# x loaded behind the embeddings' weights, gates on column tiles, two small steps moved: a change to a two-layer decoder trunk

## The chip, the cores and the metric

The kernel runs on one core of a Trainium2 chip. The metric is device time in microseconds (us) of one execution. The engines are called as the profile calls them: PE (TensorE matmul), PEld (its weight loads), DVE (VectorE), ACT (ScalarE), POOL (GpSimd), SP (SyncE, which issues most DMAs).

## The reference

256 tokens of width 2048 go through two layers. Everything is f32.

```
h = x
for i in 0, 1:
    hn = rmsnorm(h)
    if i == 0:                                   # even layer
        q, f, i, z, xb, zb = split(hn @ e_w_in)  # six blocks of 1024
        ya = head_rmsnorm(hgrn2(q, f, i)) * silu(z)       # gated linear recurrence, 8 heads of 128
        xc = causal_conv(xb)                               # 4 taps
        yb = rg_lru(xc) * silu(zb)   # r, i = sigmoid(xc @ block-diagonal), a = exp(-8 r softplus(-lam))
        h += concat(ya, yb) @ e_w_out
    else:                                        # odd layer
        qk, v, og, z, ig, fg = split(hn @ o_w_in)  # ig, fg: one column for each of 8 heads
        q, k = silu(causal_conv(qk))
        li, lf = ig + c_b_i, log_sigmoid(fg + c_b_f)
        yc = head_rmsnorm(mlstm(q, k, v, li, lf)) * sigmoid(og) * silu(z)  # cumulative sums and running
        h += yc @ o_w_out                                                    # maxima of li, lf weight q k^T
    h += sigmoid(h @ ple_gate_w[i]) * rmsnorm(p[i] @ ple_w[i])   # p: per-layer embeddings, width 256
return rmsnorm(h)
```

## The kernel before

About 200 MB of f32 weights pass once through the core. `load_weights` (L113) fetches a 1 MB tile of weights in two halves on SP's queue (L122), ACT casts each half to a rounded type (L124, `whi`), and DVE subtracts to get the low part (L125, `wlo`). Activations are split the same way (`ahl`: L139 and L140 for p, L277 and L278 with the norm's gain). Every product with a large weight is then three products, high by high, high by low, low by high. `block` does it for one column block of 128 outputs and all 256 tokens: sixteen matmuls at L155, a `pump()`, sixteen at L161. `project_tok` does it for 512 outputs with tokens on the partitions (L196, L197, L198), four quarters of the weight, a `pump()` in each.

The order of the work around these streams is written by hand. Side work is put into generators, in lanes (`start("par", ...)`, `"norm"`, `"att"`, `"rg"`, `"mix"`, `"fm"`). Each `pump()` advances every lane by one step up to its next `yield`, and holds what it issues behind the latest main instruction of PE, ACT and DVE (`tc.issue_after`). So a step's place in the stream is set by counting yields. A scheduler orders the rest of the program at build time by data and priority; casts of weights have high priority.

The stages, in order: `ple` computes the embeddings' product for layer 0 (L144 to L146, weights `pw`, result `pl` copied out at L322 and L324); `i_proj` (256 tokens by 1024, weights `ei`, twice), in whose first four quarters `load_x` also fetches x (`xq`), splits it (L277, L278) and sums its squares (L269, L272, L273); `f_proj`, `q_proj`, `xb_proj`, the gates and output projection of layer 0; then layer 1 likewise.

Four places matter here.

- `load_x(i)` (L406) issues the DMA of a quarter of x and the work on it, called by `project_tok` in front of each quarter of `ei`. `prm` (the small parameters) is loaded between the two halves of the embeddings' work.
- `derive` (L464), in lane "par", computes the lower bound of the forget gate and, after a `yield`, the decay of RG-LRU: softplus by a polynomial on [128 x 8] tiles (L481 to L495, names `ez`, `z`, `pol`, `sp`). It runs beside `i_proj`, where the `norm` lane also computes the reciprocal square root of the token norms (L204 to L233), a product of which (L236) spreads it.
- `attention(g)` (L533), in lane "att", builds the intra-chunk products level by level (L556 on 32-wide column tiles, then L625 for 32 and 64 wide), copies them into `A` (L638), and then does the product of the two halves of a chunk (L643, into `mx`, copied at L645) and `read_out`. PSUM tiles `mx` come from a pool of three buffers. `rg_lru(r)` (L693), in lane "rg", allocates `mx` tiles for its gate products (L704, read by ACT at L708), and ends with the scan at L726.
- The mLSTM's gates: 16 columns of the weight (`ogf`) are put, as high and low parts, into 128-column tiles of zeros (L828 to L835), and 32 matmuls of 256 columns multiply them with the split activations (L839). `gate_stats`, in lane "mix", adds high and low part, applies norm and bias, and computes log-sigmoid, cumulative sum, running maximum and a stabiliser (L854 to L867), on [8 x 256]. `split8` splits the maximum into high and low (L244, L245); three pumps later L876 transposes two rows, and `spread` (L252, L253) broadcasts a head's row to 128 partitions with a product with one column of `identr`.

Of the kernel before, what the change touches and what calls it, by code (L numbers as in the profile page):

```python
# [19 lines left out]
P = 128  # L20
# [16 lines left out]
    PRM[_n] = (_o, _w)  # L37
    _o += _w
NPRM = _o
NCST = 128 + 32 + 16 + 2 * 48 + 256  # L40


@with_exitstack
def trunk(ctx: ExitStack, tc: tile.TileContext, a, out):
# [58 lines left out]
    tri2 = cst[:, c0:c0 + 256]  # L103

    def pc(name, i=0, n=None):
        o, w = PRM[name]
# [3 lines left out]
        return pc(name, 0, PRM[name][1])  # L110


    def load_weights(src, pieces=1):  # L113
        parts = []
        for hf in range(2):
            raw = wp.tile([P, 1024], F32, name="raw", tag="raw", bufs=5)
            hi = wp.tile([P, 1024], F32R, name="whi", tag="whi")
            lo = wp.tile([P, 1024], F32R, name="wlo", tag="wlo")
            n = 1024 // pieces
            for c in range(0, 1024, n):  # L120
                r, h, l = (x[:, c:c + n] for x in (raw, hi, lo))
                sy.dma_start(out=r, in_=src[:, hf * 1024 + c:hf * 1024 + c + n])  # L122
                with tc.high_priority(offset=400):
                    last["act"] = s.copy(h, r).ins  # L124
                    last["dve"] = v.tensor_tensor(out=l, in0=r, in1=h.bitcast(F32), op=ALU.subtract).ins  # L125
            parts.append((hi, lo))
            pieces = 1
        return parts
# [7 lines left out]
    def split_act(src, name):  # L136
        hi, lo, both = act_pair()
        src = src.rearrange("p (k t) -> p k t", k=2)
        s.copy(hi, src)  # L139
        v.tensor_tensor(out=lo, in0=src, in1=hi.bitcast(F32), op=ALU.subtract)  # L140
        return hi, lo, both
# [94 lines left out]
        te.matmul(st[:, 0:T], ones[:, 0:P], dg, start=True, stop=True)  # L236
        return st[:, 0:T]

    def split8(x, name):

        n = x.shape[0]
        hi = tp.tile([8, T], F32R, name=name + "h", tag="s8h", bufs=1)[0:n, :]
        lo = tp.tile([8, T], F32R, name=name + "l", tag="s8l", bufs=1)[0:n, :]
        v.tensor_copy(hi, x)  # L244
        v.tensor_tensor(out=lo, in0=x, in1=hi.bitcast(F32), op=ALU.subtract)  # L245
        return hi, lo

    def spread(o, parts, h):

        n = parts[0].shape[0]  # L250
        w = identr[0:n, h:h + 1].to_broadcast([n, P])
        te.matmul(o, w, parts[0], start=True, stop=False)  # L252
        te.matmul(o, w, parts[1], start=False, stop=True)  # L253
# [48 lines left out]
    def load_p(i):  # L302
        praw = tp.tile([P, 512], F32, name="praw", tag="hn", bufs=3)
        sy.dma_start(out=praw, in_=a["pT"][i])
        return split_act(praw, "p")

    def ple(pact, pool, between):
        pls = []
        for b in range(2):
            parts = load_weights(a["pw"][b], 2 if b == 0 else 1)  # L310
            if b == 1:
                between()
            for j in range(4):
                hi, lo = parts[j // 2]
                pl = pool.tile([P, 512], F32, name="pl", tag="pl", bufs=8)
                ps = pm.tile([P, 512], F32, name="mm", tag="mm")
                for jj in range(2):
                    for k in range(2):
                        c = ((j % 2) * 4 + jj * 2 + k) * P
                        mm3(ps[:, jj * T:(jj + 1) * T], hi[:, c:c + P], lo[:, c:c + P], pact, k, k == 0, k == 1)  # L320
                if j % 2:
                    v.tensor_copy(pl, ps)  # L322
                else:
                    s.copy(pl, ps)  # L324
                pls.append(pl)
        return pls
# [71 lines left out]
    p0 = l0.enter_context(tc.tile_pool(name="p0", bufs=8))  # L398
    m0_scope = ExitStack()
    m0 = m0_scope.enter_context(tc.tile_pool(name="m0", bufs=2))  # L400
    pls = ple(load_p(0), p0, lambda: sy.dma_start(out=prm, in_=a["prm"]))
    identr = cp.tile([8, 8], F32R, name="identr")
    acc = cp.tile([P, 512], F32, name="acc", tag="acc")
    acth = []

    def load_x(i):  # L406
        t = m0.tile([P, 1024], F32, name="xq", tag="fq"[i % 2])
        sy.dma_start(out=t, in_=a["xT"][:, i * 1024:(i + 1) * 1024])
        xq.append(t)
        for j in (2 * i, 2 * i + 1):  # L410
            acth.append(gained(pair_of(xq, j), "en", j))
            add_square(gp if j < 6 else v, acc, pair_of(xq, j), j == 0)
        if i == 3:
            start("norm", finish_norm([folded(acc)], 0))
# [49 lines left out]
    def derive():  # L464
        sy.dma_start(out=cst, in_=a["cst"])
        yield
        yield

        v.tensor_tensor(out=mx, in0=pall("lg0"), in1=pall("lg1"), op=ALU.max)
        v.tensor_tensor(out=e0, in0=pall("lg0"), in1=mx, op=ALU.subtract)  # L470
        v.tensor_tensor(out=e1, in0=pall("lg1"), in1=mx, op=ALU.subtract)
        s.activation(e0, e0, AF.Exp)
        s.activation(e1, e1, AF.Exp)
        v.tensor_tensor(out=e1, in0=e0, in1=e1, op=ALU.add)
        v.reciprocal(e1, e1)
        v.tensor_tensor(out=lb, in0=e0, in1=e1, op=ALU.mult)
        v.tensor_scalar(omb, lb, -1.0, 1.0, op0=ALU.mult, op1=ALU.add)
        yield

        lam = pall("lam")  # L480
        s.activation(ez, lam, AF.Abs)  # L481
        s.activation(ez, ez, AF.Exp, scale=-1.0)
        v.tensor_scalar(z2, ez, 2.0, None, op0=ALU.add)
        v.reciprocal(z2, z2)
        v.tensor_tensor(out=ez, in0=ez, in1=z2, op=ALU.mult)
        v.tensor_tensor(out=z2, in0=ez, in1=ez, op=ALU.mult)
        v.tensor_scalar(pol, z2, 1.0 / 17.0, 1.0 / 15.0, op0=ALU.mult, op1=ALU.add)
        for c in (13, 11, 9, 7, 5, 3, 1):
            v.tensor_tensor(out=pol, in0=pol, in1=z2, op=ALU.mult)
            v.tensor_scalar(pol, pol, 1.0 / c, None, op0=ALU.add)  # L490
        v.tensor_tensor(out=pol, in0=pol, in1=ez, op=ALU.mult)
        v.tensor_scalar(sp, lam, -1.0, 0.0, op0=ALU.mult, op1=ALU.max)
        v.scalar_tensor_tensor(sp, pol, 2.0, sp, op0=ALU.mult, op1=ALU.add)
        v.tensor_scalar(sp8, sp, 8.0, None, op0=ALU.mult)
        v.tensor_scalar(spm8, sp, -8.0, None, op0=ALU.mult)  # L495

    start("par", derive())


    with m0_scope:  # L500
# [39 lines left out]
        def attention(g):  # L540
# [78 lines left out]
            for B in (32, 64):  # L619
# [17 lines left out]
                for x in range(0, P, 2 * B):  # L637
                    v.tensor_copy(A[x:x + B, :, x + B:x + 2 * B],  # L638
                                  ps.rearrange("p (c b) -> p c b", c=8)[x:x + B, :, 0:B])
                yield  # L640
            ps = px.tile([P, 512], F32, name="mx", tag="mx")
            for c in range(4):
                te.matmul(ps[:, c * P:(c + 1) * P], k[:, c * T:c * T + P], q[:, c * T + P:(c + 1) * T],  # L643
# [139 lines left out]
    l0.close()  # L783


    v.tensor_copy(identr, ident[0:8, 0:8])
    norm.clear()
    start("norm", finish_norm(accs, 2))

    with tc.tile_pool(name="m1", bufs=2) as m1:  # L790
# [29 lines left out]
            vts.append(vt)  # L820
        drain("norm")

        gr = m1.tile([P, KT, 16], F32, name="gr", bufs=1)
        sy.dma_start(out=gr, in_=a["ogf"])
        ps = pm.tile([P, 512], F32, name="mm", tag="mm")
        for hf in range(2):
            wt = wp.tile([P, 1024], F32R, name="whi", tag="whi")
            gp.memset(wt.bitcast(F32), 0.0)  # L828
            w3 = wt.rearrange("p (k c) -> p k c", c=P)
            f3 = wt.bitcast(F32).rearrange("p (k c) -> p k c", c=P)  # L830
            for w in range(2):
                src = gr[:, hf * 8:(hf + 1) * 8, w * 8:(w + 1) * 8]
                c = w * 32
                s.copy(w3[:, :, c:c + 8], src)
                v.tensor_tensor(out=w3[:, :, 64 + c:72 + c], in0=src, in1=f3[:, :, c:c + 8], op=ALU.subtract)  # L835
            for kk in range(8):
                k = hf * 8 + kk
                for i, x in enumerate(acth[k // 2][0:2]):
                    te.matmul(ps[:, 0:T], wt[:, kk * P:(kk + 1) * P], x[:, k % 2],  # L839
                              start=(k == i == 0), stop=(k == KT - 1 and i == 1))  # L840

        def t8(name):
            return m1.tile([8, T], F32, name=name, bufs=1)
# [3 lines left out]
        aT = m1.tile([P, 32], F32, name="aT", bufs=1)  # L847
        pM = []

        def gate_stats(ps):  # L850
            cbi = prm[0:8, PRM["cbi"][0]:PRM["cbi"][0] + 1]
            cbf = prm[0:8, PRM["cbf"][0]:PRM["cbf"][0] + 1]
            for x, c, b in ((li, 0, cbi), (xf, 32, cbf)):
                s.copy(x, ps[c:c + 8, 0:T])  # L854
                v.tensor_tensor(out=x, in0=x, in1=ps[64 + c:72 + c, 0:T], op=ALU.add)
                v.tensor_tensor(out=x, in0=x, in1=norm["rs"][0:8], op=ALU.mult)
                v.tensor_scalar(x, x, b, None, op0=ALU.add)
            s.activation(ab, xf, AF.Abs)
            s.activation(ab, ab, AF.Exp, scale=-1.0)
# [19 lines left out]
        start("mix", gate_stats(ps))  # L879

        SC = 0.25 * 128.0 ** -0.5
        nums = {}
# [260 lines left out]
def _const():  # L1143
# [9 lines left out]
    for b in (2, 8):  # L1153
# [3 lines left out]
        c[:, o:o + 48] = (sl // (4 * b) == n) & (sl % (4 * b) // b == np.array([0, 1, 2, 0, 1, 0])[x // b])  # L1157
        o += 48
    c[:, o:o + P] = np.where(si <= np.arange(P)[None, :], 0.0, -1e30)
    return c  # L1160


# [70 lines left out]
```

## Time and profile before

| | |
|---|---|
| time, median of 3 runs | 1079.89 us (1078.7 to 1081.84) |
| profiled execution | 1082.2 us, span from first to last instruction 1080.4 us |
| mean granted PE clock | 0.996 of full speed |
| PE / DVE / ACT / POOL busy | 98% / 69% / 54% / 12% of the span |
| DMA | 200.26 MB, mean 185 GB/s |

The rows quoted below are of this one execution. A row of the timeline has start, duration (us), engine, line, operation, output <- inputs and shape, the number of records, and in brackets the idle time of the engine just before and what ended it. A PE record ends when its modelled pipeline does, so consecutive records overlap; the distance between starts is what counts. A plain f32 product leaves two records.

### The profile page before, as it was taken

The numbers are of one execution on the slowest core, as the hardware profiler recorded it, in microseconds if no ns is written. First come the engines' busy times: TensorE is split into PE (matmuls) and PEld (weight loads), VectorE is DVE, ScalarE is ACT, GpSimd is POOL, SyncE is SP. The second block draws the span as 40 slices with busy tenths as digits, with TensorE's granted clock in tenths as the row PEclk, the third lists the DMA queues.
The fourth block names the chain that finished last, engine by engine and source line by source line (L and its number), as shares of the span: only waits on it lengthen the run. The fifth ranks groups of instructions, "written<-read, shape, count | busy, mean of one in ns | idle before, by whom it ended". The sixth has DMA issues, their size and how long they took to land.

```text
span 1080.4 us, 15904 instructions
## 1 busy us (share of the span) xinstructions
PE 1060.6 (98%) x6042; PEld 912.9 (84%) x6042; DVE 748.2 (69%) x1087; ACT 579.9 (54%) x852; POOL 131.6 (12%) x103
## 2 busy tenths in 40 slices
PE   7999999999999999999999999999999999999996
PEld 7788888878888888888888888888888888888886
DVE  6958987987777556777544877764456677655665
ACT  7565545857654435556444766554444466434543
POOL 2143542521000000112000000000000005000111
PEclk9999999999999999999999999999999999999999
DMA  8555553533755555555554544445555765554542
GB/s 317 202 205 177 175 186 134 195 131 126 277 197 183 193 195 185 190 189 184 194 195 158 193 156 157 156 166 195 194 190 187 239 217 180 192 191 173 185 176 79
DMA packets 55948, 200.26 MB, mean 185 GB/s; under 512 B 6208, under 2 KB 6464, under 8 KB 55872
## 3 DMA queue, kind: packets, MB, share of 16 engines
q1 hardware_dynamic: 54720, 195.06, 51.5%
q0 software_dynamic: 1152, 4.19, 1.1%
q8 instruction: 47, 0.77, 0.3%
q14 instruction: 29, 0.24, 0.1%
HBM read 197.13 MB, written 2.10 MB: 184 GB/s over the span
## 4 chain that ended last, share of the span: by engine, by line
PE 92%; DVE 4%; ACT 1%; issue 1%; DMA 0%; SPq 0%; DVEq 0%; ACTq 0%
PE mm L155 32%; PE mm L161 17%; PE mm L196 12%; PE mm L197 12%; PE mm L198 12%; DVE wlo L125 2%; DVE ahl L278 1%; PE mm L1082 1%; PE mm L1081 1%; PE mm L1080 1%; PE nu L918 1%; DMA raw<-in_pw_dram 0%; PE mx L444 0%; PE mx L556 0%; ACT whi L124 0%
## 5 line engine op out<-in xcount | busy, mean ns | idle before, releaser
L125 DVE TENSOR_TENSOR wlo<-raw,whi 128x1024 fp32r<-128x1024 f32 (+1 forms) x361 | 455.5, 1286 | 237.1 <-ACT whi L124 136.6
L124 ACT CAST whi<-raw 128x1024 fp32r<-128x1024 f32 (+1 forms) x361 | 377.1, 1048 | 330.3 <-PE mm L155 158.0
L155 PE MATMUL mm<-ahl,whi 128*128 128x512 f32 x1536 | 367.2, 391 | 0.0
L155 PEld LDWEIGHTS mm<-ahl,whi 128*128 128x128 f32 x1536 | 282.1, 188 | 56.1 <-DVE ahl L278 0.7
L196 PE MATMUL mm<-whi,ahl 128*128 128x512 f32 x608 | 239.4, 394 | 0.0
L197 PE MATMUL mm<-wlo,ahl 128*128 128x512 f32 x608 | 236.8, 390 | 1.1 <-DVE wlo L125 1.1
L198 PE MATMUL mm<-whi,ahl 128*128 128x512 f32 x608 | 236.8, 390 | 0.0
L161 PE MATMUL mm<-ahl,wlo 128*128 128x256 f32 x1536 | 202.1, 284 | 0.0
L161 PEld LDWEIGHTS mm<-ahl,wlo 128*128 128x128 f32 x1536 | 195.5, 191 | 6.7
L197 PEld LDWEIGHTS mm<-wlo,ahl 128*128 128x128 f32 x608 | 114.3, 188 | 24.5 <-DVE wlo L125 1.5
L198 PEld LDWEIGHTS mm<-whi,ahl 128*128 128x128 f32 x608 | 114.1, 188 | 23.9
L196 PEld LDWEIGHTS mm<-whi,ahl 128*128 128x128 f32 x608 | 114.3, 188 | 23.4
L167 ACT COPY sm<-mm 128x256 f32<-128x256 f32 x64 | 23.6, 369 | 41.5 <-PE mm L161 41.5
L273 POOL TENSOR_TENSOR acc<-acc,sq 128x512 f32<-128x512 f32 x11 | 17.4, 1580 | 215.4 <-ACT sq L272 215.2
L980 POOL DMA_DIRECT2D row<-in_rows_dram x4 | 2.1, 537 | 285.0 <-DVE u L970 264.9
L168 DVE TENSOR_TENSOR mg<-mm,sm 128x256 f32<-128x256 f32 x64 | 26.6, 415 | 0.1
L803 DVE SCALAR_TENSOR_TENSOR qk<-mg,prm,qk 128x255 f32<-128x255 f32 (+2 forms) x48 | 21.3, 480 | 6.8 <-ACT qk L800 6.5
L1068 POOL TENSOR_TENSOR pl<-pl,row 128x512 f32<-128x512 f32 x6 | 9.2, 1533 | 134.5 <-ACT sq L1052 134.5
L1080 PE MATMUL mm<-whi,ahl 128*128 128x256 f32 x64 | 18.3, 285 | 0.0
L1082 PE MATMUL mm<-whi,ahl 128*128 128x256 f32 x64 | 18.1, 283 | 0.0
L1081 PE MATMUL mm<-wlo,ahl 128*128 128x256 f32 x64 | 18.1, 283 | 0.0
L178 DVE TENSOR_TENSOR mg<-mg,hrs 128x512 f32<-128x512 f32 (+1 forms) x25 | 17.7, 707 | 0.5
(292 smaller groups left out, 825.9 us busy)
## 6 DMA issues: line engine op xcount, KB each, us to landing
raw<-in_ew_dram SPq DMA_DIRECT2D x64, 512.0 KB, 4.3
raw<-in_g_dram SPq DMA_DIRECT2D x56, 512.0 KB, 3.7
raw<-in_eo_dram SPq DMA_DIRECT2D x32, 512.0 KB, 4.0
raw<-in_ov_dram SPq DMA_DIRECT2D x32, 512.0 KB, 3.7
raw<-in_oqk_dram SPq DMA_DIRECT2D x32, 512.0 KB, 4.1
raw<-in_oog_dram SPq DMA_DIRECT2D x32, 512.0 KB, 3.8
raw<-in_oz_dram SPq DMA_DIRECT2D x32, 512.0 KB, 3.8
raw<-in_oo_dram SPq DMA_DIRECT2D x32, 512.0 KB, 3.9
```

The costliest lines, as they stand in the source:

```text
L124: last["act"] = s.copy(h, r).ins
L125: last["dve"] = v.tensor_tensor(out=l, in0=r, in1=h.bitcast(F32), op=ALU.subtract).ins
L155: last["pe"] = te.matmul(ps, parts[k // 8][0][:, c:c + P], act[k // 2][2][:, (k % 2) * 512:(k % 2 + 1) * 512], start=(k == 0), stop=False).ins
L161: last["pe"] = te.matmul(ps[:, T:2 * T], parts[k // 8][1][:, c:c + P], act[k // 2][0][:, k % 2], start=False, stop=(k == KT - 1)).ins
L167: s.copy(small, ps[:, T:2 * T])
L168: v.tensor_tensor(out=dst, in0=ps[:, 0:T], in1=small, op=ALU.add)
L196: te.matmul(ps[hf], xh, wh, start=(k == 0), stop=False)
L197: te.matmul(ps[hf], xh, wl, start=False, stop=False)
L198: last["pe"] = te.matmul(ps[hf], xl, wh, start=False, stop=(k == KT - 1)).ins
L1080: te.matmul(ps[hf], xh, wh, start=(k == 0), stop=False)
L1081: te.matmul(ps[hf], xh, wl, start=False, stop=False)
L1082: last["pe"] = te.matmul(ps[hf], xl, wh, start=False, stop=(k == KT - 1)).ins
```

## The change

1. **Start.** `load_weights` takes a list of queues; the first half of the embeddings' weights comes in four DMAs of 256 columns, in turn from ACT's queue and SP's. The four quarters of x are all issued right behind `prm`, and `load_x` no longer issues a DMA, so the weights of `i_proj` come behind x. The embeddings' matmuls are tied to program order (`issue_after`), and the split of p gets high priority.
2. **Softplus.** The decay becomes a generator of its own, `decay`, started in lane "par" after `attention(0)`.
3. **Cross-half product.** For g = 1 a further `yield` stands in front of it.
4. **Gates.** The weight's gain is multiplied in (DVE), and sixteen plain f32 matmuls of 32 output columns on four column tiles take the unsplit activations `hq`; each column tile gets the sum over a quarter of the 16 blocks. A copy (`gm`) and one product with a 0/1 matrix `gsum` (40 more columns of `cst`) add the four; this product is one pump later than the old first step. `split8` becomes `split_rows`: high and low rows lie in one [40 x 256] tile, so `spread` is one product instead of two.

```
-    def load_weights(src, pieces=1):
+    def load_weights(src, pieces=1, queues=(sy,)):
...
-                sy.dma_start(out=r, in_=src[:, hf * 1024 + c:hf * 1024 + c + n])
+                queues[(hf * 1024 + c) // n % len(queues)].dma_start(out=r, in_=src[:, hf * 1024 + c:hf * 1024 + c + n])
...
+    def split_rows(x):
+        both = tp.tile([40, T], F32R, name="s8", tag="s8", bufs=1)
+        v.memset(both.bitcast(F32), 0.0)
+        v.tensor_copy(both[0:8], x)
+        v.tensor_tensor(out=both[32:40], in0=x, in1=both[0:8].bitcast(F32), op=ALU.subtract)
+        return both
+
+    def spread(o, both, h):
+        te.matmul(o, identr[:, h:h + 1].to_broadcast([40, P]), both, start=True, stop=True)
...
     def load_p(i):
-        return split_act(praw, "p")
+        with tc.high_priority(offset=0 if i else 800):
+            return split_act(praw, "p")
...
-            parts = load_weights(a["pw"][b], 2 if b == 0 else 1)
+            parts = load_weights(a["pw"][b], *((4, (s, sy)) if b == 0 else ()))
...
-                        mm3(ps[:, jj * T:(jj + 1) * T], hi[:, c:c + P], lo[:, c:c + P], pact, k, k == 0, k == 1)
+                        with ExitStack() as behind:
+                            if "pe" in last:
+                                behind.enter_context(tc.issue_after(last["pe"]))
+                            mm3(ps[:, jj * T:(jj + 1) * T], hi[:, c:c + P], lo[:, c:c + P], pact, k, k == 0, k == 1)
...
-    pls = ple(load_p(0), p0, lambda: sy.dma_start(out=prm, in_=a["prm"]))
+    def early_loads():
+        sy.dma_start(out=prm, in_=a["prm"])
+        for i in range(4):
+            t = m0.tile([P, 1024], F32, name="xq", tag="fq"[i % 2])
+            sy.dma_start(out=t, in_=a["xT"][:, i * 1024:(i + 1) * 1024])
+            xq.append(t)
+
+    pls = ple(load_p(0), p0, early_loads)
...
     def load_x(i):
-        t = m0.tile([P, 1024], F32, name="xq", tag="fq"[i % 2])
-        sy.dma_start(out=t, in_=a["xT"][:, i * 1024:(i + 1) * 1024])
-        xq.append(t)
...
+    def decay():
         lam = pall("lam")
...
+        yield
...
                 yield
+            if g:
+                yield
             ps = px.tile([P, 512], F32, name="mx", tag="mx")
             for c in range(4):
                 te.matmul(ps[:, c * P:(c + 1) * P], k[:, c * T:c * T + P], q[:, c * T + P:(c + 1) * T],
...
         start("att", attention(0))
+        start("par", decay())
...
+        wt = m1.tile([P, KT, 32], F32, name="wt", tag="wt", bufs=1)
+        gp.memset(wt, 0.0)
+        v.tensor_tensor(out=wt[:, :, 0:16], in0=gr, in1=pall("on").unsqueeze(2).to_broadcast([P, KT, 16]), op=ALU.mult)
         ps = pm.tile([P, 512], F32, name="mm", tag="mm")
-        for hf in range(2):
...
-                for i, x in enumerate(acth[k // 2][0:2]):
-                    te.matmul(ps[:, 0:T], wt[:, kk * P:(kk + 1) * P], x[:, k % 2],
-                              start=(k == i == 0), stop=(k == KT - 1 and i == 1))
+        for k in range(KT):
+            c = 32 * (k % 4)
+            te.matmul(ps[c:c + 32, 0:T], wt[:, k], pair_of(hq, k // 2)[:, (k % 2) * T:(k % 2 + 1) * T],
+                      start=(k < 4), stop=(k >= KT - 4))
+        gm = m1.tile([P, T], F32, name="gm", bufs=1)
+        s.copy(gm, ps[:, 0:T])
...
-        def gate_stats(ps):
+        def gate_stats():
+            yield
+            ps = px.tile([P, 512], F32, name="mx", tag="mx")
+            te.matmul(ps[0:40, 0:T], gsum, gm, start=True, stop=True)
...
-                s.copy(x, ps[c:c + 8, 0:T])
-                v.tensor_tensor(out=x, in0=x, in1=ps[64 + c:72 + c, 0:T], op=ALU.add)
-                v.tensor_tensor(out=x, in0=x, in1=norm["rs"][0:8], op=ALU.mult)
+                v.tensor_tensor(out=x, in0=ps[c:c + 8, 0:T], in1=norm["rs"][c:c + 8], op=ALU.mult)
...
-            pM.append(split8(Mx, "Mx"))
+            pM.append(split_rows(Mx))
```

More of the change, by code (lines that the diff above doesn't have):

```diff
@@ L39 @@
 NPRM = _o
-NCST = 128 + 32 + 16 + 2 * 48 + 256
+NCST = 128 + 32 + 16 + 2 * 48 + 256 + 40
 @with_exitstack
@@ L103, in trunk @@
     tri2 = cst[:, c0:c0 + 256]
+    c0 += 256
+    gsum = cst[:, c0:c0 + 40]
     def pc(name, i=0, n=None):
@@ L237, in to_free @@
         return st[:, 0:T]
[L239 to L253, printed above, removed]
+    def split_rows(x):
[6 more added lines that the diff above has]
+        te.matmul(o, identr[:, h:h + 1].to_broadcast([40, P]), both, start=True, stop=True)
     def folded(acc, *more):
@@ L400, in trunk @@
     m0 = m0_scope.enter_context(tc.tile_pool(name="m0", bufs=2))
-    pls = ple(load_p(0), p0, lambda: sy.dma_start(out=prm, in_=a["prm"]))
-    identr = cp.tile([8, 8], F32R, name="identr")
+    def early_loads():
[5 more added lines that the diff above has]
+    pls = ple(load_p(0), p0, early_loads)
+    identr = cp.tile([40, 8], F32R, name="identr")
     acc = cp.tile([P, 512], F32, name="acc", tag="acc")
@@ L783, in trunk @@
     l0.close()
-    v.tensor_copy(identr, ident[0:8, 0:8])
+    v.memset(identr.bitcast(F32), 0.0)
+    for c in (0, 32):
+        v.tensor_copy(identr[c:c + 8], ident[0:8, 0:8])
     norm.clear()
@@ L824, in trunk @@
         sy.dma_start(out=gr, in_=a["ogf"])
+        wt = m1.tile([P, KT, 32], F32, name="wt", tag="wt", bufs=1)
+        gp.memset(wt, 0.0)
+        v.tensor_tensor(out=wt[:, :, 0:16], in0=gr, in1=pall("on").unsqueeze(2).to_broadcast([P, KT, 16]), op=ALU.mult)
         ps = pm.tile([P, 512], F32, name="mm", tag="mm")
-        for hf in range(2):
[L827 to L837, printed above, removed]
-                for i, x in enumerate(acth[k // 2][0:2]):
-                    te.matmul(ps[:, 0:T], wt[:, kk * P:(kk + 1) * P], x[:, k % 2],
-                              start=(k == i == 0), stop=(k == KT - 1 and i == 1))
+        for k in range(KT):
[4 more added lines that the diff above has]
+        s.copy(gm, ps[:, 0:T])
         def t8(name):
@@ L877, in gate_stats @@
             v.tensor_copy(aT, px_[:, 0:32])
-        start("mix", gate_stats(ps))
+        start("mix", gate_stats())
         SC = 0.25 * 128.0 ** -0.5
@@ L1159, in _const @@
     c[:, o:o + P] = np.where(si <= np.arange(P)[None, :], 0.0, -1e30)
+    o += 256
+    for h in range(8):
+        c[:, o + h] = si[:, 0] % 32 == h
+        c[:, o + 32 + h] = si[:, 0] % 32 == 8 + h
     return c
```

## The prediction, made before the changed kernel ran

> **What bounds the kernel now.** I read the page's busy times first, then its chain, then all that TensorE (PE) waited for.
>
> ```profile
> PE 1060.6 (98%) x6042; PEld 912.9 (84%) x6042; DVE 748.2 (69%) x1087; ACT 579.9 (54%) x852; POOL 131.6 (12%) x103
> PE 92%; DVE 4%; ACT 1%; issue 1%; DMA 0%; SPq 0%; DVEq 0%; ACTq 0%
> PE mm L144 <- ACT whi L124: 6.8, 2, 5.6
> PE mx L643 <- DVE A L638: 2.0, 1, 2.0
> PE mm L197 <- DVE wlo L125: 1.1, 1, 1.1
> PE st L236 <- DVE dg L233: 0.8, 1, 0.8
> ```
>
> The first line is busy time by engine, the second the share of each engine in the chain that ended last. The other four are the whole answer to what PE waited for: in total, times, longest. PE is the bound: a dense stream in a fixed order with four holes (start, 29.98, 49.07, 238.01). So an edit can pay in two ways only: it closes a hole or takes matmuls out of the stream. It can cost by opening a new hole, or by putting matmuls in. Work moved between VectorE (DVE), ScalarE (ACT) and GpSimd (POOL) costs nothing as long as no hole opens. The profiled run took 1082.2 us against a median of 1079.89. I sum against the profiled run and carry the difference to the median.
>
> **1. The start: x behind the embedding weights, these in four pieces, matmuls in program order.**
>
> ```profile
> 4.94 0.62 ACT L124 CAST whi<-raw 128x512 fp32r<-128x512 f32 x1 [0.88 <-DMA raw<-in_pw_dram]
> 6.95 0.62 ACT L124 CAST whi<-raw 128x512 fp32r<-128x512 f32 x1 [1.39 <-DMA raw<-in_pw_dram]
> ...
> 15.18 0.51 ACT L277 ACTIVATE ahl<-xq,prm 128x256 fp32r<-128x256 f32 x1
> 15.59 0.62 ACT L269 ACTIVATE acc<-xq 128x512 f32<-128x512 f32 x1
> 16.11 1.03 ACT L124 CAST whi<-raw 128x1024 fp32r<-128x1024 f32 x1
> ```
> ```profile
> 5.61 0.58 PE L144 MATMUL mm<-ahl,whi 128*128 128x256 f32 x1 [5.61 <-ACT whi L124]
> ...
> 13.76 0.30 PE L144 MATMUL mm<-ahl,whi 128*128 128x256 f32 x1
> ...
> 21.69 0.40 PE L196 MATMUL mm<-whi,ahl 128*128 128x512 f32 x1
> ...
> 29.98 0.50 PE L197 MATMUL mm<-wlo,ahl 128*128 128x512 f32 x1 [1.07 <-DVE wlo L125]
> ```
>
> (Start, length, engine, line, operation; in brackets the idle time before it and what ended it.) The two pieces of the first half have landed by 4.94 and 6.95. The old order puts a matmul of the second piece third, so PE waits a second time for L144: 6.8 − 5.6 = 1.2 us. With pieces of half the size, the first lands half of 2.0 us earlier (first matmul near 4.6), and in program order the second wait goes. That is 2.2 us in all. The clock runs half at first: from 5.61 to 13.76, less the 1.2, 30 matmuls take 0.23 each; the 66 from 13.76 to 21.69 take 0.12. About as many slow ones stay if the clock rises as long after the start as now, so the 96 matmuls of the embeddings end near 19.5: up to −2.2 by themselves.
>
> But the weights of i_proj now stand behind all four pieces of x, in the DMA stream and on ACT. Their first cast was at 16.11. On ACT's new order there are ahead of it in addition six scaled copies (0.41 each, 15.18 to 15.59), two squares (0.52, 15.59 to 16.11) and two L324 copies of the squares' size: 6 × 0.41 + 4 × 0.52 = 4.5 us. Two of these come back, by the earlier start and by ACT's waits for data in front of 15.18. The cast falls near 19.2 to 20.5, with 1.03 of its own. The low half (L125 on DVE) then stands behind the last embedding copy as well: I take 21.6, the later end. L196 can run once before that, so i_proj effectively starts at about 21.3 instead of 21.69. **−0.4**; bounds −2.2 (the weights are in time) and +1.3 (the cast another 1.7 later, as ACT's order has it if x lands late).
>
> Behind that the four pieces of x are already cast, and ACT and DVE, which worked through them between the weights of i_proj, have that time free. The hole at 29.98 (1.07, and a matmul of 0.50 in place of 0.40) goes: **−1.2**, bounds −1.3 and 0.
>
> **2. The decay's softplus moves from i_proj to behind attention(0).**
>
> ```profile
> 46.20 0.16 DVE L490 TENSOR_SCALAR pol<-pol 128x8 f32<-128x8 f32 x1
> ...
> 48.59 0.42 DVE L233 TENSOR_TENSOR dg<-cst,rcr 128x256 f32<-128x256 f32 x1
> ```
> ```profile
> 49.07 0.70 PE L236 MATMUL st<-dg,ones 128*128 128x256 f32 x2 [0.84 <-DVE dg L233]
> ```
> ```profile
> 80.00:100.00 20.00, 20.00 (x114) 17.53 (x113) 18.78 (x47) 11.86 (x16) 3.02 (x1) 1.00 0.57 180
> ```
>
> (The last row is a window: length, then busy PE, weight loads, DVE, ACT, POOL, then clock, DMA share, GB/s.) The decay's 24 small operations (46.20 is one: 0.16, about 0.2 with the gap to the next) stand ahead of and between the steps of the square-root chain that ends with L233, for which L236 waits 0.84. Without them DVE comes to L233 earlier by 24 × 0.16 = 3.8 us if nothing else holds it, far more than 0.84. The hole closes; with the change of form on both sides staying, **−0.9**, bounds −1.1 and 0. The same 3.8 us and two table loads on ACT come back near 80 to 100, where DVE is busy 18.78 of 20. PE shows no hole there: the waits above list a single L197 in the whole run. I take 0, since that lead hides them. If DVE has no lead, it falls 3.8 − 1.2 = 2.6 behind: bound +2.6. Nothing but the decay's own steps queues behind its waits, and its result is used first at 200, by RG-LRU.
>
> **3. The cross-half product one pump later (g = 1).**
>
> ```profile
> 233.15 2.28 DVE L726 TENSOR_TENSOR_SCAN tt<-av,it 128x1024 f32<-128x1024 f32 x1
> ...
> 237.18 0.68 DVE L638 COPY A<-mx 64x512 f32<-64x512 f32 x1
> ```
> ```profile
> 238.01 1.13 PE L643 MATMUL mx<-f,k 128*128 128x128 f32 x8 [2.01 <-DVE A L638]
> 238.98 3.52 PE L704 MATMUL mx<-xc,bw 128*128 128x256 f32 x8
> ```
> ```profile
> 240.00:241.00 1.00, 1.00 (x3) 0.75 (x3) 0.00 (x0) 0.76 (x3) 0.00 (x0) 0.50 0.36 111
> ```
>
> L643 does not read A. It waits for the PSUM buffer that L638 empties (three buffers in rotation), and L638 stands on DVE behind the scan and L125. After the change, the next product that asks for a buffer at this pump is the gate product of RG-LRU, L704. It is issued there as before, takes the same buffer, and DVE's order is unchanged. So the hole moves from L643 to L704 and keeps its size: **0**, bounds −4.1 (below) and +0.5. Read-out(1) comes one pump later; its users come later still.
>
> After the hole the window at 240 shows clock 0.50, and eight records of L704 take 3.52 instead of 1.99 (row at 200.70 below): 1.5 us lost, and by a few neighbours up to 1.9. Hole and clock are worth 4.1 with the broken pitch. The Trainium skill ("TensorE: Matmul & The Clock Gate", "Why this matters for your kernels") asks for no idle gaps over about 3 us, and has one idle window send the clock back; here 2.0 us idle were enough, so the trace differs. By the page the hole would cost itself alone, 2.2.
>
> **4. Gates on column tiles.**
>
> ```profile
> 588.03 4.00 PE L839 MATMUL mm<-ahl,whi 128*128 128x256 f32 x32
> 591.86 2.46 PE L155 MATMUL mm<-ahl,whi 128*128 128x512 f32 x10
> 122.17 1.29 PE L155 MATMUL mm<-ahl,whi 128*128 128x512 f32 x5
> 123.39 0.89 PE L556 MATMUL mx<-q,k 128*32 128x48 f32 x64
> 124.21 2.17 PE L161 MATMUL mm<-ahl,wlo 128*128 128x256 f32 x16
> 200.70 1.99 PE L704 MATMUL mx<-xc,bw 128*128 128x256 f32 x8
> 202.34 2.26 PE L161 MATMUL mm<-ahl,wlo 128*128 128x256 f32 x16
> 619.27 0.27 PE L253 MATMUL mx<-Mxl,identr 8*128 8x256 f32 x1
> 619.38 0.27 PE L252 MATMUL mx<-Mxh,identr 8*128 8x256 f32 x1
> ```
> ```profile
> 606.62 0.41 DVE L245 TENSOR_TENSOR Mxl<-Mx,Mxh 8x256 fp32r<-8x256 f32 x1
> ```
>
> Before: 588.03 to 591.86, 3.83 us on the path. After: sixteen plain f32 products of 256 columns. One of these costs (202.34 − 200.70) / 4 = 0.41 (L704: four products, two records each). Do four column tiles run at once? L556 says so: its 32 products of 48 columns would need 32 × 0.41 × 48/256 = 2.5 in sequence and take 124.21 − 123.39 = 0.82, three to one. Four rounds of 0.41 are 1.64. Into and out of the tiled form I add 0.3: five L155 at 0.23 from 122.17 end near 123.3, so L556 starts 0.09 late, and leaving costs twice as much. 1.9 against 3.83: **−1.9**, bounds −2.2 (no change of form) and +3.1 (all in sequence: 6.6 + 0.3). The same page of the Trainium skill (Part 3, on packing) gives 2.38 for three column tiles; by that figure the sixteen would take 2.8, an estimate, the term be −0.7 and the whole 1076.8, inside the forecast's own spread below.
>
> The new sum over tiles is one f32 product more, 0.41, and its change of form: **+0.6**, bounds +0.4 and +0.8. Spread takes two matmuls instead of four per pair of heads, 0.11 each (619.27 to 619.38), four pairs: **−0.9**.
>
> Waits: the gate chain began at 592.0 (end of L839) and ended at 607.03 (L245): 15.0, twelve us ahead of the spread at 619. The sum over tiles now stands in the second block's pump, on a clock of before 591.86 + 5.6 + 3.7 = 601.1 (a block is sixteen L155 at 0.23 and sixteen L161 at 0.12). With 15.0 the chain ends at 616.1, three us ahead; but in DVE's new order more merges and convolutions stand between its steps, and I get up to 4.7 us more. So it is late by nothing to 1.7. **+0.4**, bounds 0 and +1.7.
>
> **Sum:** −0.4 − 1.2 − 0.9 + 0 − 1.9 + 0.6 − 0.9 + 0.4 = −4.3 us. Profiled 1082.2 becomes 1077.9; the median 1079.89 becomes 1075.6.
>
> **Rivals.**
> - *The hole at 238 really closes*: L638 comes in time for L704. −4.1 more: 1071.5. For: L638 is late by 2.0 only, and everything before it runs on an altered schedule of loads. Against: DVE's order and L704's place are as before.
> - *A new wait at the fifth block.* The gate chain is late by 1.7, and the idle time halves the clock for a window, 1.7 more, less the 0.4 allowed: 1078.6. For: a lead of three us against an uncertainty of 4.7. Against: nothing in the old trace waits in this stretch.
> - *i_proj starts badly.* PE's idle time before 21.6 adds up to some 2 us, the clock falls (1.7), and the start gains nothing (0.4): 1077.7; with the cast 1.7 later still, 1079.4. For: 2.0 us idle did it at 238. Against: here it comes in two parts.
> - *The column tiles do not overlap* (the other side). The term is +3.1 instead of −1.9: −4.3 + 5.0 = +0.7, 1080.6; and if each of 16 changes of tile costs the 0.09 seen at 123.39, +2.1, 1082.0. It decides as soon as the sixteen take over 6.2 us, fewer than 1.1 at a time. For: no row shows tiles at 256 columns. Against: three to one at 48 columns, where a fixed cost would weigh more. The Trainium skill ("TensorEngine Tiling (Array Packing)", "Key Properties") says that a change of tiling mode drains the engine, a change of tile does not; the 0.09 at 123.39 agrees with a short drain.
>
> That an edit does nothing is in the forecast: the later product.
>
> **How the numbers follow.** Forecast 55%, hole at 238 gone 12%, new wait 13%, bad start 10%, tiles in sequence 10%. Three tenths of a percent, about what a measurement of this kernel can tell from no change, are 3.2 us: faster is below 1076.7, slower above 1083.1. The forecast's own spread, ±2 from unknown costs and the phase of the clock's windows, puts about three quarters of its 55% there: 0.42; with 0.12 of the closed hole and 0.06 of the two waits, 0.6. Slower needs the tiles in sequence or DVE behind at 80 to 100 together with one of the waits: 0.1. The rest, 0.3, lies within. Range 1071.0 to 1081.0: from the closed hole to past the tiles in sequence; it leaves out half of these two, about 1 in 10, and the tails.
>
> **What would show it.** First PE matmul before 5, L196's first near 20.5 with a wait near 1 on L125, no wait at 30 or 49; L704 waiting 2.0 on L638 near 235 and half clock in the next windows; the column-tile line 2 us long in fours; a wait of 0 to 1.7 at the spread near 613. I am wrong if the tile line takes over 3 us, if PE shows holes between 80 and 115, or if PE's total of matmuls plus holes falls by less than two.

## The result, and the profile after

| | before | after |
|---|---|---|
| median of 7 runs | 1080.19 us (1078.7 to 1081.84) | 1086.11 us (1082.85 to 1086.38) |
| ratio, 95% interval | | 1.0049 [1.0035, 1.0063] |
| profiled execution, span | 1082.2, 1080.4 | 1086.06, 1084.3 |

Slower by half a percent; a gain of 4.3 us was forecast, and the time lies above the range. The page's busy times and all that PE waited for, of the kernel after (columns as before the change):

```profile
PE 1060.5 (98%) x6036; PEld 910.8 (84%) x6036; DVE 748.4 (69%) x1087; ACT 580.2 (54%) x851; POOL 129.6 (12%) x102
...
PE mm L146 <- ACT ahl L141: 5.2, 1, 5.2
PE mx L566 <- DVE q L571: 5.1, 1, 5.1
PE mx L716 <- DVE A L648: 2.0, 1, 2.0
PE mm L199 <- DVE wlo L127: 1.4, 1, 1.4
PE mm L198 <- ACT whi L126: 0.9, 1, 0.9
```

The busy sums are almost equal and do not show the loss. The waits show it. A new one of 5.1 us stands second. Line numbers have moved: L566 is the first column-tile product of attention (L556 before), L571 the multiplication that makes its input (L561), L716 RG-LRU's gate product (L704), L648 the copy of attention's tile (L638), L127 the low half of a weight (L125), L198 to L200 `i_proj` (L196 to L198), L542 q's projection (L532), L499 the polynomial (L490).

Aligning PE's stream matmul by matmul gives the ledger of the two profiled executions (minus is earlier than before):

| part | forecast | measured |
|---|---|---|
| start and the hole at 29.98 | −1.6 | +0.1 |
| hole at the norm's spread | −0.9 | −1.1 |
| softplus where it went, with the clock behind the hole | 0 | +7.0 |
| cross-half product | 0 | −0.1 |
| gates on column tiles | −1.9 | −1.8 |
| sum over tiles, spread, new wait | +0.1 | −0.2 |
| sum | −4.3 | +3.9 |

The sum of +3.9 is less than the 5.9 between the medians, since the profiled execution before (1082.2 us) was longer than its median of 1080.19.

The large term on VectorE, timeline of the kernel after:

```profile
110.32 4.55 DVE L127 TENSOR_TENSOR wlo<-raw,whi 128x1024 fp32r<-128x1024 f32 x2
114.80 0.41 DVE L170 TENSOR_TENSOR mg<-mm,sm 128x256 f32<-128x256 f32 x1
115.13 0.93 DVE L492 TENSOR_SCALAR z<-ez 128x8 f32<-128x8 f32 x1
...
119.18 0.17 DVE L499 TENSOR_SCALAR pol<-pol 128x8 f32<-128x8 f32 x1
119.28 2.36 DVE L127 TENSOR_TENSOR wlo<-raw,whi 128x1024 fp32r<-128x1024 f32 x2
121.56 0.42 DVE L170 TENSOR_TENSOR mg<-mm,sm 128x256 f32<-128x256 f32 x1
...
122.01 0.69 DVE L180 TENSOR_TENSOR mg<-mg,hrs 128x512 f32<-128x512 f32 x1
...
123.38 1.22 DVE L127 TENSOR_TENSOR wlo<-raw,whi 128x1024 fp32r<-128x1024 f32 x1
124.51 0.48 DVE L542 SCALAR_TENSOR_TENSOR q<-mg,omb,th 128x256 f32<-128x256 f32 x1
124.91 1.22 DVE L127 TENSOR_TENSOR wlo<-raw,whi 128x1024 fp32r<-128x1024 f32 x1
126.04 0.48 DVE L542 SCALAR_TENSOR_TENSOR q<-mg,omb,th 128x256 f32<-128x256 f32 x1
126.44 0.42 DVE L170 TENSOR_TENSOR mg<-mm,sm 128x256 f32<-128x256 f32 x1
126.77 0.68 DVE L571 TENSOR_TENSOR q<-q,f 128x512 f32<-128x512 f32 x1
```

Eighteen operations of the softplus run from 115.13 to 119.28, and six more between 121.90 and 123.38. Behind them in VectorE's queue come the last weight halves and merges of `q_proj(0)`, q itself (L542) and L571. The same stretch before the change:

```profile
119.63 0.69 DVE L178 TENSOR_TENSOR mg<-mg,hrs 128x512 f32<-128x512 f32 x1
121.03 0.88 DVE L532 SCALAR_TENSOR_TENSOR q<-mg,omb,th 128x256 f32<-128x256 f32 x2 [0.70 <-ACT th L528]
121.94 0.69 DVE L561 TENSOR_TENSOR q<-q,f 128x512 f32<-128x512 f32 x1
```

L561 ended at 122.63, and its reader L556 started at 123.39 without a wait. The lead that was there was thus 0.76 us. After the change L571 ends at 127.45. On PE, timeline and windows of the kernel after (length, busy PE, PEld, DVE, ACT, POOL, clock, DMA share, GB/s):

```profile
127.51 1.51 PE L566 MATMUL mx<-q,k 128*32 128x48 f32 x64 [5.08 <-DVE q L571]
```
```profile
127.40:131.70 4.30, 4.19 (x77) 4.08 (x78) 1.95 (x5) 0.00 (x0) 1.51 (x1) 0.50 0.48 162
132.00:136.00 4.00, 4.00 (x22) 3.33 (x21) 4.00 (x7) 2.12 (x3) 0.64 (x1) 1.00 0.47 153
```

The hole costs 5.1. Three numbers make it: L571 ends 4.8 us later than L561 did (127.45 against 122.63), PE arrives 1.0 earlier by the ledger, and the lead of 0.76 covers a part (4.8 + 1.0 − 0.76). Half clock behind the hole costs 1.9 more: by the ledger's alignment the delay grows from 4.1 at L566's first record to 6.0 at 134.

### The profile page after: what moved, and what is told of

Its sections match the earlier page's. It is cut to its first block, busy times and chain, and to the rows that moved or that the text cites. A ratio compares the mean times of both kernels' runs of the same rounds, so it can differ in the third digit from the quotient of the medians.

```text
span 1084.3 us, 15885 instructions
## 1 busy us (share of the span) xinstructions
PE 1060.5 (98%) x6036; PEld 910.8 (84%) x6036; DVE 748.4 (69%) x1087; ACT 580.2 (54%) x851; POOL 129.6 (12%) x102
## 4 chain that ended last, share of the span: by engine, by line
PE 91%; DVE 4%; ACT 2%; issue 1%; DMA 1%; DVEq 0%; SPq 0%; ACTq 0%
PE mm L157 30%; PE mm L163 16%; PE mm L199 12%; PE mm L198 12%; PE mm L200 12%; DVE wlo L127 2%; PE mm L1093 1%; PE mm L1091 1%; PE mm L1092 1%; DMA xq<-in_xT_dram 1%; PE nu L929 1%; PE mx L451 0%; PE mx L566 0%; ACT whi L126 0%; DVE xc L750 0%
## 5 line engine op out<-in xcount | busy, mean ns | idle before, releaser
L127 DVE TENSOR_TENSOR wlo<-raw,whi 128x1024 fp32r<-128x1024 f32 (+1 forms) x363 | 455.0, 1278 | 244.9 <-ACT whi L126 144.4
L198 PE MATMUL mm<-whi,ahl 128*128 128x512 f32 x608 | 240.2, 395 | 0.9 <-ACT whi L126 0.9
L200 PE MATMUL mm<-whi,ahl 128*128 128x512 f32 x608 | 237.4, 390 | 0.0
L198 PEld LDWEIGHTS mm<-whi,ahl 128*128 128x128 f32 x608 | 114.5, 189 | 24.4 <-ACT whi L126 1.1
L200 PEld LDWEIGHTS mm<-whi,ahl 128*128 128x128 f32 x608 | 114.7, 189 | 24.1
L170 DVE TENSOR_TENSOR mg<-mm,sm 128x256 f32<-128x256 f32 x64 | 26.5, 415 | 0.1
L275 ACT ACTIVATE ahl<-mx,prm 128x256 fp32r<-128x256 f32 x24 | 11.0, 473 | 13.8 <-PE mx L451 7.9
```

Source lines behind the costliest of these rows:

```text
L170: v.tensor_tensor(out=dst, in0=ps[:, 0:T], in1=small, op=ALU.add)
L198: te.matmul(ps[hf], xh, wh, start=(k == 0), stop=False)
L200: last["pe"] = te.matmul(ps[hf], xl, wh, start=False, stop=(k == KT - 1)).ins
```

## Experiments

Theory A: the softplus operations stand in VectorE's queue in front of q and L571, and that, with the clock, is the loss. Rivals: ScalarE's part of the softplus with its table loads (B); another part of the change (C). All ratios are to the kernel before on the same chip, with a 95% interval.

**Softplus back in `derive`, the rest as changed.**
```
-    def decay():
-        lam = pall("lam")
+        lam = pall("lam")        # in derive again, behind its last yield
...
-        start("par", decay())
```


> The changed kernel with the decay's softplus back where it was (in derive, beside i_proj). Theory A (VectorE's queue: the softplus operations stand in front of the last q operations of q_proj(0) and of L571, for which the first column-tile product of attention(0) waits 5.1 us, and the half clock behind that hole costs 1.9): hole and half clock go, the hole of about 1.0 at the spread of the norm comes back: 1086.1 - 7.0 + 1.0 = 1080.1 us. Rival C (the hole comes from another part, such as loads that arrive at other times behind the new start): the hole stays, about 1087.

Measured: 1078.65 us, 0.9984 [0.9973, 0.9994]. The hole and the half clock behind it are gone, C falls. But the hole at the norm's spread did not come back: PE's waits list only the start, i_proj's two and the copy. The earlier start closes it by itself, as the run with part 1 alone below confirms.

**Softplus in i_proj(1).**
```
     start("par", derive())
+    start("par", decay())
...
     def decay():
+        yield
+        yield
...
-        start("par", decay())
```


> The changed kernel with the softplus two pumps later than before the change, in i_proj(1), where VectorE is about half busy (2.45 of 5 us). Theory A: no hole at 127 and none at the spread of the norm, 1086.1 - 7.0 = 1079.1 us. Rival C: the hole at 127 stays, 1086.

Measured: 1077.7 us, 0.9981 [0.9970, 0.9991]. VectorE runs the 24 operations from 48.13 to 54.71, fourteen of them in the window from 50 to 55. It is 4.37 us busy there, and PE does not wait:

```profile
50.00:55.00 5.00, 5.00 (x24) 4.14 (x23) 4.37 (x16) 2.11 (x2) 0.00 (x0) 1.00 0.50 143
```

**The softplus move alone, on the kernel before.**
```
     (before)
+    def decay():
...
         start("att", attention(0))
+        start("par", decay())
```


> The kernel before with the softplus moved as in the change and nothing else. Theory A: the hole at the spread of the norm closes (-1.0), a hole of about 5 us at the first column-tile product of attention(0) opens and the clock falls behind it (+7.0): 1080.2 + 6.0 = 1086.2 us. Rival C (the hole needs another part of the change as well): 1079.2.

Measured: 1087.68 us, 1.0058 [1.0039, 1.0078], with the hole of 5.1 at the same product. The move alone makes the loss.

**Only VectorE's operations moved.**
```
+        s.activation(ez, pall("lam"), AF.Abs)            # in derive
+        s.activation(ez, ez, AF.Exp, scale=-1.0)
...
     def decay():
-        s.activation(ez, lam, AF.Abs)
-        s.activation(ez, ez, AF.Exp, scale=-1.0)
```


> The changed kernel, but ScalarE's two steps of the softplus (Abs and Exp, and so the two extra table loads) stay in derive; only the VectorE operations run behind attention(0). Theory A (the VectorE operations make the hole): hole of 4.5 to 5.2 us stays, 1085.5 to 1086.1 us. Rival B (ScalarE's table loads of 1.28 us each, and VectorE waiting in order for ScalarE, make a good part of it): hole smaller by 1.3 to 2.6 us, 1083 to 1084.5.

Measured: 1081.6 us, 1.0017 [1.0008, 1.0027]. PE's wait and VectorE's timeline:

```profile
PE mx L566 <- DVE q L571: 2.6, 1, 2.6
```
```profile
122.10 0.69 DVE L180 TENSOR_TENSOR mg<-mg,hrs 128x512 f32<-128x512 f32 x1
...
123.49 0.88 DVE L542 SCALAR_TENSOR_TENSOR q<-mg,omb,th 128x256 f32<-128x256 f32 x2
124.40 0.69 DVE L571 TENSOR_TENSOR q<-q,f 128x512 f32<-128x512 f32 x1
```

Theory A missed the size. B came out right in the size of the hole, but neither in time (1081.6 against 1083 to 1084.5) nor in mechanism. The VectorE operations by themselves leave a hole of 2.6 us. The other 2.4 is order: L180 ends at nearly the same time in both (122.7 and 122.8), but here the two L542 and L571 follow as soon as the polynomial is done, while with ScalarE's steps in the stretch two L127 and an L170 stand between them (1.2 + 1.2 + 0.4 in the rows above, overlapping a little). In the kernel after, ScalarE's second table load itself ran early and held up nothing, as ScalarE waited 5.29 for VectorE behind it:

```profile
116.16 1.28 ACT L538 ACT_TABLE_LOAD   x1
122.74 0.63 ACT L538 ACTIVATE th<-mg 128x512 f32<-128x512 f32 x1 [5.29 <-DVE mg L180]
```

The order is fixed when the program is built. That the scheduler reckoned with the table load there, and so put the weight halves ahead, fits, but was not shown by itself.

**Part 3 undone, on the softplus in i_proj(1).**
```
-            if g:
-                yield
```


> As e2, without the added pump ahead of the second cross-half product (part 3 undone). Theory A (the hole near 236 belongs to the PSUM buffer, not to the product): the wait of 2.0 us on the same copy moves from RG-LRU's gate product back to the cross-half product, the time stays within 0.5 us of e2, 1077.7. Rival (the later product is worth something by itself): 1079 or more.

Measured: 1078.5 us, 0.9975 [0.9963, 0.9988], against 0.9981 with the pump. In microseconds this lies between the two expectations, but the kernel before ran 1.3 us longer on this chip (1081.41 against 1080.1); the ratios do not differ. The wait is the same 2.0 on the same copy, and only changes its line:

```profile
PE mx L656 <- DVE A L651: 2.0, 1, 2.0
```

**Copies ahead on VectorE, on the softplus in i_proj(1).**
```
+                with tc.high_priority(offset=400):
                     for x in range(0, P, 2 * B):
                         v.tensor_copy(A[x:x + B, :, x + B:x + 2 * B], ...)
```


> As e2 (softplus in i_proj(1), 1077.7 us), and the copies out of attention's PSUM tiles for 32 and 64 wide products get priority on VectorE's queue, so that the one for which a gate product of RG-LRU waits 2.0 us stands ahead of the convolution and the scan. Theory A (the product that comes next in the pool inherits the wait, whichever it is; the wait is the copy's place in VectorE's queue): the hole of 2.2 us near 236 and the half clock behind it (1.3 to 1.9) go, 1073.8 to 1075.5 us. Rival (another wait is right behind, such as ScalarE's reading of the third buffer): the hole stays above 1 us, 1076.5 or more.

Measured: 1077.3 us, 0.9967 [0.9956, 0.9978]; the interval overlaps that of 0.9981. The wait on the copy is gone, and another takes its place, one product later:

```profile
234.68 1.03 PE L720 MATMUL mx<-xc,bw 128*128 128x256 f32 x4
237.44 1.13 PE L720 MATMUL mx<-xc,bw 128*128 128x256 f32 x4 [1.73 <-ACT av L724]
```
```profile
235.25 1.28 ACT L724 ACT_TABLE_LOAD   x1 [2.04 <-DVE tt L742]
236.55 0.84 ACT L724 ACTIVATE av<-mx,prm 128x256 f32<-128x256 f32 x2
```

The gate products get their first two buffers, and then wait for ScalarE to read them. ScalarE waited for the scan (L742) and loads a table first. So the rival was right: of 2.2 us, 0.3 remain as gain in PE's stream (the hole's excess is 1.9). The clock stayed full behind it in this execution.

**Two quarters of x ahead instead of four, on the softplus in i_proj(1).**
```
-        for i in range(4):
+        for i in range(2):                      # in early_loads
...
     def load_x(i):
+        if i >= 2: (tile and dma_start of quarter i)
```


> As e2, but only the first two quarters of x are issued ahead of i_proj's weights, the other two between them as before the change. Theory A (work on x stands ahead of the first cast of i_proj's weights on ScalarE): the stalls of 1.0 and 1.4 us at the start of i_proj shrink below 0.5 together and the half clock of 1.6 goes, while up to 1.2 of the old hole at 30 may come back: 1074 to 1076.5 us against 1077.7. Rival (the stalls come from the DMA stream or from the embedding copies): stalls stay within 0.5 of 2.4, 1077.2 to 1078.2.

What it answers to, in the kernel after, timelines of PE, ScalarE and VectorE:

```profile
19.76 0.73 PE L198 MATMUL mm<-whi,ahl 128*128 128x512 f32 x2 [0.87 <-ACT whi L126]
21.91 0.50 PE L199 MATMUL mm<-wlo,ahl 128*128 128x512 f32 x1 [1.41 <-DVE wlo L127]
```
```profile
17.68 0.62 ACT L270 ACTIVATE sq<-xq 128x512 f32<-128x512 f32 x1
18.20 0.57 ACT L326 COPY pl<-mm 128x512 f32<-128x512 f32 x1
18.66 1.05 ACT L126 CAST whi<-raw 128x1024 fp32r<-128x1024 f32 x1
```
```profile
20.04 0.68 DVE L324 COPY pl<-mm 128x512 f32<-128x512 f32 x1
20.64 2.34 DVE L127 TENSOR_TENSOR wlo<-raw,whi 128x1024 fp32r<-128x1024 f32 x2
```
```profile
22.60:25.90 3.30, 3.30 (x10) 2.52 (x9) 3.30 (x4) 3.00 (x5) 3.03 (x2) 0.50 0.86 273
```

The cast of i_proj's first weights runs at 18.66 and its low half from 20.64, behind x's work and the last embedding copy. PE stalls twice, and the clock is half from 22.6 to 25.9. With two quarters of x ahead: 1076.27 us, 0.9962 [0.9950, 0.9975]. Both stalls are gone, and i_proj runs 3.5 us earlier than with the softplus in i_proj(1) alone. The old hole at 30 did not come back, but in the profiled execution a wait that was not expected, of the norm for GpSimd, gives all of the 3.5 back by 44.4, with half the clock behind it. The median lies in theory A's range all the same:

```profile
40.77 0.61 PE L225 MATMUL st<-ones,acc 128*128 128x1 f32 x4 [1.57 <-POOL acc L254]
```
```profile
41.50:44.50 3.00, 3.00 (x8) 2.35 (x8) 2.40 (x15) 0.32 (x1) 0.00 (x0) 0.50 1.00 393
```

**Gates on one column tile, in sequence, on the softplus in i_proj(1).**
```
-            c = 32 * (k % 4)
+            c = 0                                # all sixteen summed in one PSUM tile
...
-                      start=(k < 4), stop=(k >= KT - 4))
+                      start=(k == 0), stop=(k == KT - 1))
```


> As e2, but all sixteen gate products go to one column tile (output partitions 0 to 31) in sequence, summed there. Theory A (four column tiles run at once): the stretch of the gates grows from about 1.9 to 16 x 0.43 = 6.9 us, +5.0, 1082.7 us. Rival (the time falls because plain products on 32 columns are cheap by themselves): the stretch stays below 4 us, 1079.8 or less.

Measured: 1084.11 us, 1.0022 [1.0008, 1.0035]. The line on PE, on four tiles (kernel after) and on one:

```profile
594.14 1.93 PE L847 MATMUL mm<-hq,wt 128*32 128x256 f32 x32
```
```profile
587.51 7.09 PE L849 MATMUL mm<-hq,wt 128*32 128x256 f32 x32
```

Four column tiles at 256 columns are 7.09 / 1.93 = 3.7 times as fast as one. On one tile the plain products take longer than the 3.83 us of the old form, so the rival falls: the gain of the gates is all concurrency.

**Parts 1 and 4 alone, on the kernel before** (their hunks of the diff, nothing else).

> The kernel before with part 1 alone (embedding weights in four pieces from two queues, program order, x ahead of i_proj's weights). Theory A, from the two traces: up to the norm's spread the part gains 0.1 and no more, because i_proj's stalls and the half clock behind them (-2.9 + 1.0 + 1.6 + 1.6 - 1.2) give back what the start won: 1079.5 to 1081 us, no change. As predicted: -1.6, 1078.5.

> The kernel before with part 4 alone (gates on column tiles, sum over tiles, spread in one product). Theory A, from the two traces: gates -1.8, sum over tiles +0.5, spread -0.7, no new wait: -2.0 us, 1078.1. Rival (the sum over tiles one pump later makes the chain late when the stages before it run without delay): 0 to +1.5, with a wait at the fifth block.

Measured: the start 1080.37 us, 1.0000 [0.9988, 1.0013]; the gates 1077.87 us, 0.9976 [0.9964, 0.9989]. The start is worth nothing in the median, with two stalls (0.3 and 1.4 us, against 0.9 and 1.4 in the kernel after). In its profiled execution the clock did not fall behind these stalls, and the stream is 1.5 us shorter than before, 1.0 of this from the hole at the norm's spread. The gates are worth 2.6 us by the ratio, and 2.1 from the first gate product to the end by the stream, with no wait at the fifth block.

**Put together, twice.** Both have the softplus in i_proj(1) and the copies first.
```
     # first: quarters 0 and 1 of x early, 2 and 3 both in load_x(1)
...
     # second: quarters 0 and 1 early, 2 and 3 each in its load_x, and
-            add_square(gp if j < 6 else v, acc, pair_of(xq, j), j == 0)
+            add_square(gp if j < 5 else v, acc, pair_of(xq, j), j == 0)
```


> e5 (softplus in i_proj(1), the copies first) with two quarters of x ahead of i_proj's weights and the other two right behind the first quarter of these. Theory A: the stalls at the start of i_proj go as in e6 (-4 with the half clock), and with the last quarters of x one step earlier the wait of the norm on GpSimd's sum (1.6 in e6) goes too; the price is the casts for x ahead of the second quarter of i_proj's weights, up to 1 us. From e5's 1077.3: 1073.3 to 1074.5 us. Rival (the work on x only moves its hole along): 1076 or more, with a hole at the second quarter of i_proj or at the norm.

> e5 with e6's order of loads, and one of the sums of squares moved from GpSimd to VectorE. Theory A: no stall at the start of i_proj (-4), wait at the norm 0.5 to 1.6 us: 1074 to 1075.5 us. Rival (GpSimd's fold waits for the last sum on VectorE, not for its own sums): wait at the norm stays at 1.6, 1075.5.

Measured: the first 1078.5 us, 0.9978 [0.9967, 0.9990], the second **1073.13 us, 0.9938 [0.9918, 0.9957]** in four runs, the fastest here and a little below both its expectations. The first moves the hole to the second quarter of i_proj, as its rival said:

```profile
28.49 0.50 PE L199 MATMUL mm<-wlo,ahl 128*128 128x512 f32 x1 [3.29 <-DVE wlo L127]
```

In the second, PE's waits are the very first matmul and ScalarE's reading of the gate products, no others; the wait at the norm, expected at 0.5 us at least, is gone:

```profile
PE mm L146 <- ACT ahl L141: 5.2, 1, 5.2
PE mx L724 <- ACT av L728: 1.7, 1, 1.7
```

## Why the prediction was wrong

- **The step that failed is in part 2**: "I take 0, since that lead hides them". The lead was inferred from weight halves, for which PE never waits there. What had no lead was another reader of VectorE's queue: L561 and its 0.76 us. It is never listed as a wait, since PE did not wait by 0.76 us. I also priced the move by the window 80 to 100, while the operations ran at 115 to 123. They are started behind `attention(0)`, and its first product, L556, stands at 123.39 in the prediction's own rows; the sign that it named, holes between 80 and 115, looked too early for the same reason. "Nothing but the decay's own steps queues behind its waits" was false: q, L571 and the weight halves do. The price was low as well: 24 × 0.16 = 3.8 leaves out the gaps, with which the prediction itself gives 0.2 for one operation, so 4.8; the 24 took 4.8 us of busy time. And the bound of +2.6 was VectorE's busy time alone. It left out the order that changes around the inserted work (2.4 us, by the run with ScalarE's steps left behind) and the half clock (1.9).
- **Part 1 was mis-sized** (−1.6 forecast, +0.1 in the ledger, nothing in the median of the run of its own). The mechanism, stalls of i_proj behind x's work, was forecast, with stalls of about 1 each; they were 0.87 and 1.41 us. The first cast ran at 18.66, ahead of the 19.2 to 20.5 that was forecast (its own 16.11 + 4.5 − 2 gives 18.6), yet `i_proj` came no earlier than before. What was given to a rival at one in ten, the halved clock behind the stalls, cost 1.6 in the profiled execution. The embeddings started at 5.2, not 4.6.
- **The hole at the norm's spread** closed as forecast, but by part 1: with the softplus back in its place it stayed closed. With part 2 alone it closed too. So the moved softplus bought nothing in this change.
- **Part 3 was right**: RG-LRU's gate product inherits the wait, 2.0 before and after.
- **Part 4 was right**: 1.8 against 1.9 for the gates, and no wait of the gate chain (+0.4 was allowed). The estimate of 2.8 us, worked out from the figure of the Trainium skill ("TensorE: Matmul & The Clock Gate", Part 3) for three column tiles, was too long for four: they took 1.93 us, 3.7 times as fast as one; the trace decides.

The rivals listed a hole at 238 that closes and tiles in sequence. VectorE behind stood only as a bound and, together with another wait, inside the tenth for a slower kernel. What happened had no chance of its own.

## What to carry to other kernels

A list of waits shows where there is no lead, never how much there is elsewhere. Before work is put into an in-order queue, take each operation behind the new place and measure the time from its end to the start of its reader; the smallest is the room, here 0.76 us for 4.8 us of small operations. Pauses of the queue on the way to that reader can add to it, here one of 0.70 at L532. Look by windows for a stretch where the engine is idle (VectorE is busy for only 2.45 of 5 us in i_proj(1)) and move the work there. Where a product waits for a buffer, moving the product leaves the wait to the next one: move what empties the buffer, and look at what empties the one after it.

## What the runs showed of the hardware

- **The clock behind a hole depends on where the hole falls.** A wait of 1.57 us (two quarters of x) was followed by 3 us at clock 0.50. One of 3.29 us (first put-together, profiled execution) was not. In the clock records of the traces, every stretch at half clock behind a hole lasts 3.41 us or twice that, and the stretches at full clock in front of it and between are whole multiples of 3.41. Cut into stretches of 3.41 counted from the first rise of the clock, the wait of 3.29 falls into two of them (first two rows), and the 2.0 at 238 in the kernel before into one (last row):

```profile
23.54:26.95 3.41, 1.66 (x8) 1.04 (x6) 3.36 (x7) 3.41 (x6) 1.98 (x2) 1.00 0.22 90
26.95:30.36 3.41, 1.87 (x8) 1.58 (x9) 3.41 (x5) 2.52 (x5) 0.00 (x0) 1.00 0.25 88
30.36:33.78 3.42, 3.42 (x17) 2.83 (x16) 3.42 (x7) 1.33 (x2) 0.00 (x0) 1.00 0.75 218
```
```profile
235.66:239.07 3.41, 1.40 (x11) 1.09 (x10) 3.00 (x4) 3.40 (x6) 0.00 (x0) 1.00 0.27 91
```

  PE is idle for 1.75 and 1.54 us in the two, and for 2.01 in the one, behind which the clock halved. Over all fourteen traces, without their starts and ends (before 12.5 us, after 1060), half clock followed each of the 18 such stretches with 1.8 us idle or more, and two of the 14 with 1.0 to 1.8 (1.57 and 1.72). The Trainium skill ("TensorE: Matmul & The Clock Gate", Part 1) has the activity window run freely, 3.4 us long; this agrees with both. The Trainium skill's advice (same page, "Why this matters for your kernels") of no gaps over about 3 us does not hold as a limit here: 2.0 in one stretch was enough, and once 1.57. The phase of the window would also explain the spread of the kernel after, whose seven runs go from 1082.85 at a mean clock of 0.996 to 1086.38 at 0.991, and that of the first put-together: its profiled execution took 1076.64 at 0.997, and eight of the ten runs 1078.2 to 1078.7 at 0.995 or 0.996. This is not shown, since only the profiled executions have traces.
- **VectorE slows beside GpSimd.** Two L127 took 4.55 us at 110.32 while GpSimd multiplied (101.21 to 116.0), and 2.36 at 119.28 after it had ended. That this is part of why `q_proj(0)` had no room is likely, but no run shows it:

```profile
101.21 14.82 POOL L349 TENSOR_TENSOR pl<-pl,plrs 128x512 f32<-128x512 f32 x8 [2.51 <-ACT plrs L262]
```
